# Attention in a hybrid layer: the products by the rows of reciprocal sums stand behind a visit's turned tiles and copies instead of behind its minima

## The chip, the core and the metric

The kernel runs on one core of a Trainium2 chip. The metric is the device time of one launch in microseconds. The core's engines run their own queues of instructions in order: TensorE (PE; its weight loads are shown as PEld), VectorE (DVE), ScalarE (ACT), GpSimd (POOL) and SyncE (SP). An instruction that waits for a semaphore holds all that is queued behind it on its engine. SP's queue issues most DMA transfers, POOL's and ACT's a few.

## The reference

One layer with two branches over the same 1024 tokens, all in float32, with 1024 channels: a projection of the normed input; branch A, a chunked state space scan (SSD); branch B, attention with a forget gate; two output projections, a merge by sigmoid gates, a last projection and a norm. What the change touches is branch B, 16 heads of 64:

```python
fcum = jnp.cumsum(log_f, axis=-1)
for blk in range(seqlen // ATT_BLOCK):
    q0, q1 = blk * ATT_BLOCK, (blk + 1) * ATT_BLOCK
    s = jnp.einsum('bhqd,bhkd->bhqk', q[:, :, q0:q1], k[:, :, :q1]) * scale
    s = s + fcum[:, :, q0:q1, None] - fcum[:, :, None, :q1]
    s = jnp.where(kpos[None, :] <= qpos[:, None], s, -jnp.inf)
    prob = jax.nn.softmax(s, axis=-1)
    outs.append(jnp.einsum('bhqk,bhkd->bhqd', prob, v[:, :, :q1]))
```

The output of each head is then multiplied by silu(z_att), the gate.

## The kernel before

**Stages.** After a prologue (norm and turned input, to about 100 us) a stream of matrix products runs to the end. Its products are made of seven products of combined blocks instead of eight (x0h to x6h in the rows; `raw` is a loaded weight block, `sum` a sum of two, `wop` its high and low parts). Into this stream the two branches are woven: the SSD groups to about 655 us, then the attention from 667 to 1143 us, then the output projections, the merge and the norm alone.

**Visits.** The attention handles its 16 heads as 8 pairs, hp 0 to 7 (both heads e of a pair lie on one tile's two halves of the partitions). A pair takes 6 visits g = 0 to 5, and visit m is 6 hp + g. A visit takes two blocks of 128 queries against one half h of 512 keys: (7, 6) half 1, (7, 6) half 0, (5, 4) half 1, (5, 4) half 0, (3, 2) and (1, 0) half 0. A set n of query blocks ends at an odd g: n = 0 at g = 1, n = 1 at g = 3 and n = 2 (the lower four blocks) at g = 5. `end(m)` gives the set that ends in visit m, if one does.

**One visit** m issues, in this order:

1. `scores`: for each of the four (block, head), PE makes s, DVE takes the row's minimum (L1526, a custom instruction and a read of its accumulator, into nm), ACT the exponential with its sum sm (L1530).
2. `out` of the set that ended two visits ago. For n = 0 and 1 it is DVE's product o*rb (L1491) and the sum of the two halves into zr (L1492); for n = 2 one product into zr (L1485). Behind n = 1 and n = 2, `outputs` stores zr to ya_dram by POOL (L1581) and makes differences for the output projections' blocks, on POOL for all pairs but the last (L1587, L1593, L1594, L1607), which are stored later as the stream's chores.
3. `weighted`: PE multiplies the previous visit's p by v into av.
4. For the set that ended one visit ago: `free`, DVE's o = av * gate (L1479), and `send`: PE turns ns (tp), ACT copies it (st, L1452), POOL stores it to st_dram (L1454).
5. For the set that ends here: `settle`, DVE's L1425 and two L1427 (the difference of the halves' minima, dd), and ACT's exponential of dd (L1428).
6. `fill(m, 0)`: a share of the stream's half steps (12 PE products each, with their weight splits on ACT L354 and DVE L356, sums L363, L379, evictions L410, L422 and the like).
7. For the set that ends here: `scale` (DVE L1439, L1440, the reciprocal L1441, ns at L1444; L1435 and L1436 for n = 2) and `load_gates` (SP loads zr from za_dram, L1466; there are two zr tiles).
8. `loads` of later tiles (v at L1399, q, k, and others), then `turned`: PE turns the exponentials (pt, L133), and the copies p leave PSUM by DVE (L1548, one block in four) or ACT (L1550).
9. For the set that ended one visit ago: `take`, SP's two loads of rb from st_dram, each row of reciprocal sums spread over 64 partitions (L1460).
10. `fill(m, 1)`: a second share of the stream.

The PSUM tiles s, pt and tp share four banks, so a visit's scores wait for the copies p of the visit before. `tc.high_priority()` and `pin` steer a list scheduler that sets each engine's order when the program is built; it goes by the order of issue and its own estimates of time. rb lies in a ring of four tiles that the stream's th tiles use too. Where a set ends in visit m, its tp is turned in m + 1, its rb asked for in m + 1, and its product made in m + 2. So the products stand in odd visits from m = 3 on.

Of the kernel before, what the change touches and what calls it, by code (L numbers as in the profile page):

```python
# [86 lines left out]
def hybrid_layer(ctx: ExitStack, tc, a, out):  # L87
# [1105 lines left out]
    with tc.tile_pool(name="pro", bufs=1, reuse_waits="tile", side="right") as pro, tc.tile_pool(  # L1193
# [44 lines left out]
        def turned(tiles, k):  # L1238
            pt = prop.tile([P, HALF], F32, tag="pt", bufs=3, name="pt")
            for j in range(4):  # L1240
                turn(pt[:, j * P : (j + 1) * P], tiles[j][:, k * P : (k + 1) * P]) 
            return pt
# [112 lines left out]
    with tc.tile_pool(name="att", bufs=1, reuse_waits="tile", side="right") as ap, tc.tile_pool(  # L1355
# [142 lines left out]
        def scores(hp, g, u):  # L1498

            pair, h = GROUPS[g]  # L1500
            i = pair[u]
            w = min(HALF, (i + 1) * P - h * HALF)
            s = [pp.tile([P, HALF], F32, tag="s", bufs=4, name="s") for e in range(2)]
            t, keys = q[hp, pair], k[hp, h]
            isl = slice(i % 2 * P, i % 2 * P + P)
            ops = [(t[:, x, isl], keys[:, y, 0:w]) for x, y in ((0, 0), (0, 1), (1, 0))]
            diagonal = h == i // 4
            for m, (x, y) in enumerate(ops):
                for e in range(2):
                    mm(  # L1510
                        s[e][:, 0:w], x[rows[e]], y[rows[e]], start=(m == 0), stop=(m == 2 and not diagonal),
                        skip_group_check=True,
                    )
            if diagonal:
                for n, (x, y) in enumerate(corner):
                    for e in range(2):
                        mm(
                            s[e][:, w - P : w], x[rows[e]], y[rows[e]], start=False, stop=(n == 1),
                            skip_group_check=True,
                        )  # L1520
            hd = heads[hp]
            for e in range(2):
                o = ex[:, e, u, 0:w]
                nm = hd.at(hd.nm, i, h, e)
                pin(
                    nc.vector.tensor_tensor_reduce(  # L1526
                        o, s[e][:, 0:w], fb[hp, h][:, e, 0:w], 1.0, 3.0e38, ALU.add, ALU.min, nm
                    )
                )
                pin(nc.scalar.activation(o, o, AF.Exp, scale=-1.0, bias=nm, accum_out=hd.at(hd.sm, i, h, e)))  # L1530
# [23 lines left out]
        def weighted(hp, g, b, first, p, start, stop):  # L1554
            pair, h = GROUPS[g]
            n = (7 - pair[0]) // 2 if pair[0] > 3 else 2
            hd = heads[hp]
            if n not in hd.av:
                hd.av[n] = pp.tile([P, HALF], F32, tag="av", bufs=1, name="av")
            c0 = 256 * h if n < 2 else pair[1] * P  # L1560
            for e in range(2):
                mm(
                    hd.av[n][rows[e], c0 + first * P : c0 + 256], v[hp, h][:, b % 4, rows[e]], p[:, e, first:, :],
                    start=start, stop=stop, skip_group_check=True,
                )
# [44 lines left out]
        def loads(m):  # L1610

            hp, g = divmod(m, 6)
            more = hp + 1 < NK
            if g == 0:
                if hp:
                    load_v(hp, 0)
                if hp < KH:
                    stream.chores += [None] + list(ops_s.differences(hp, difference_tile, small))
            if g == 1:
                load_q(hp, (3, 2))  # L1620
            if g == 2 and more:
                load_k(hp + 1, 1)
            if g == 3:
                load_q(hp, (1, 0))
                if more:
                    load_v(hp + 1, 1)
                if hp >= KH:
                    state["t"] = difference_tile()
                    nc.sync.dma_start(state["t"], ops_a.block("t1", hp - KH))
            if g == 4:  # L1630
                if more:
                    load_q(hp + 1, (7, 6))
                if hp >= KH:
                    state["y"] = fetched("b11", hp - KH)
            if g == 5 and more:
                load_k(hp + 1, 0)
                load_q(hp + 1, (5, 4))

        def end(m):

            hp, g = divmod(m, 6)
            if 0 <= hp < NK and g % 2:
                yield heads[hp], g // 2
# [15 lines left out]
        def fill(m, part):  # L1659
            share = weights[min(m // 6, NK - 1)] * rooms[m % 6][part]  # L1660
            to = stream.steps.index((ends[4], 6))
            stream.halves(round((2 * (to - stream.at) - (stream.run is not None)) * share / left[0]))
            left[0] -= share

        made = []
        for m in range(6 * NK + 1):

            stream.visit = m + 1
            hp, g = divmod(m, 6)
            if not g and hp < NK:  # L1670
                heads[hp] = Heads(hp)
            if m < 6 * NK:
                for u in range(2):
                    scores(hp, g, u)
            for hd, which in end(m - 2):
                hd.out(which)
            for one in made:
                weighted(*one)
            for hd, which in end(m - 1):
                hd.free(which)  # L1680
                if m < 6 * NK:
                    hd.send(which)
            stream.release()
            if m == 6 * NK:
                heads[NK - 1].out(2)
                stream.visit = 0
                break
            for hd, which in end(m):
                hd.settle(which)
            fill(m, 0)  # L1690

            for hd, which in end(m):
                hd.scale(which)
                hd.load_gates(which)
            loads(m)
            made = turned(hp, g)
            for hd, which in end(m - 1):
                hd.take(which)
            if m == 6 * NK - 1:
                heads[hp].send(2)  # L1700
            stream.hold()
            fill(m, 1)
            if m == 6 * NK - 1:
                heads[hp].take(2)
# [59 lines left out]
```

## Time and profile before

| | us |
|---|---|
| median of 3 runs | 1293.77 |
| the three runs | 1293.59, 1293.77, 1294.79 |
| the profiled execution, its own time | 1294.79 |
| its span | 1293.1 |
| granted TensorE clock, mean share of full | 0.997 |

The profiled execution is the slowest of the three. A row of the timeline reads: start, length, engine, line, operation, tiles (out<-in), shape, count, and in brackets the idle time of the engine ahead of it with what ended it. Idle time of an engine costs time only where the engine that sets the end waits in its turn. Other groups of instructions in the page's list, by busy time:

```profile
L356 DVE TENSOR_TENSOR wop<-sum,wop 128x512 fp32r<-128x512 f32 x174 | 140.5, 808 | 53.4 <-ACT wop L354 52.7
L1530 ACT ACTIVATE ex<-ex,nm 128x512 f32<-128x512 f32 (+1 forms) x192 | 116.1, 606 | 76.9 <-DVE nm L1526 75.7
L1526 DVE CUSTOM_DVE_ANT_0 ex<-s,fb 128x512 f32<-128x512 f32 (+1 forms) x192 | 96.8, 553 | 24.4 <-PE s L130 24.3
L130 PE MATMUL s<-k,q 64*128 64x512 f32 (+3 forms) x576 | 75.7, 373 | 6.2 <-DVE p L1548 4.4
```

Behind the first bar stand the busy time in us and the mean ns of one, behind the second the idle time of the engine ahead of the group, and what ended most of it.

### The profile page before, as it was taken

What the parts mean: (1) busy time and instruction counts of PE and PEld (TensorE: products, weight loads), DVE (VectorE), ACT (ScalarE), POOL (GpSimd) and SP (SyncE); (2) the same over time, 40 slices, a digit from 0 to 9 for tenths busy, and PEclk for the clock granted to TensorE, in tenths of its full rate; (3) what the DMA queues carried; (4) which work ended last, traced back from release to release, by engine and by line L of the source; (5) the groups of instructions that cost most, each with busy time, mean ns of one, the idle gap of its engine ahead of it and who ended that gap; (6) DMA issues with size and microseconds to landing.
All of it is one profiled execution on the core that took longest, in us unless ns stands there. A gap on an engine that the chain in (4) does not pass through costs nothing. (4 is left out here: it accounts for less than half of the span.)

```text
span 1293.1 us, 21078 instructions
## 1 busy us (share of the span) xinstructions
PE 1253.8 (97%) x7066; PEld 986.1 (76%) x7066; DVE 1014.7 (78%) x1979; ACT 794.3 (61%) x1728; POOL 284.6 (22%) x307
## 2 busy tenths in 40 slices
PE   6999999999999999899999999999999999999998
PEld 4787888788888888688776777777767777678786
DVE  6998888888789878788676766676789767876875
ACT  8755666466556756566555666566677556743654
POOL 0000330024102320143001222222121313256052
PEclk9999999999999999999999999999999999999999
DMA  7332543644363545445564657666677657665932
GB/s 281 104 106 71 154 148 121 199 140 146 127 210 116 153 153 164 122 154 154 168 237 153 221 175 224 193 208 196 228 282 250 219 178 253 230 219 189 364 112 102
DMA packets 154669, 233.60 MB, mean 181 GB/s; under 512 B 17216, under 2 KB 62656, under 8 KB 154560
## 3 DMA queue, kind: packets, MB, share of 16 engines
q1 hardware_dynamic: 142016, 205.53, 49.8%
q0 software_dynamic: 6400, 16.10, 3.3%
q10 hardware_dynamic: 6144, 10.62, 2.2%
q8 instruction: 56, 0.92, 0.3%
q14 instruction: 53, 0.43, 0.1%
HBM read 162.99 MB, written 72.34 MB: 182 GB/s over the span
## 5 line engine op out<-in xcount | busy, mean ns | idle before, releaser
L356 DVE TENSOR_TENSOR wop<-sum,wop 128x512 fp32r<-128x512 f32 x174 | 140.5, 808 | 53.4 <-ACT wop L354 52.7
L354 ACT ACTIVATE wop<-sum 128x512 fp32r<-128x512 f32 x174 | 108.8, 626 | 99.0 <-DVE sum L363 44.7
L1530 ACT ACTIVATE ex<-ex,nm 128x512 f32<-128x512 f32 (+1 forms) x192 | 116.1, 606 | 76.9 <-DVE nm L1526 75.7
L410 ACT ACTIVATE s<-pb 128x512 f32<-128x512 f32 x141 | 83.5, 592 | 97.3 <-PE pb L130 95.9
L130 PE MATMUL pc<-x3h,wop 128*128 128x512 f32 x384 | 131.6, 399 | 2.5 <-ACT wop L354 2.0
L130 PE MATMUL pb<-x0h,wop 128*128 128x512 f32 x384 | 132.2, 400 | 0.7 <-ACT x0h L1246 0.6
L130 PE MATMUL pc<-x2h,wop 128*128 128x512 f32 x384 | 131.4, 399 | 0.4 <-DVE u L422 0.4
L130 PE MATMUL pb<-x6h,wop 128*128 128x512 f32 x376 | 129.2, 399 | 1.6 <-ACT s L410 1.6
L130 PE MATMUL pb<-x5h,wop 128*128 128x512 f32 x376 | 128.3, 398 | 1.3 <-ACT s L410 1.3
L130 PE MATMUL pb<-x4h,wop 128*128 128x512 f32 x376 | 128.6, 398 | 0.2 <-DVE wop L356 0.2
L356 DVE TENSOR_TENSOR wop<-raw,wop 128x512 fp32r<-128x512 f32 x149 | 104.3, 702 | 29.8 <-ACT wop L354 29.5
L1526 DVE CUSTOM_DVE_ANT_0 ex<-s,fb 128x512 f32<-128x512 f32 (+1 forms) x192 | 96.8, 553 | 24.4 <-PE s L130 24.3
L354 ACT ACTIVATE wop<-raw 128x512 fp32r<-128x512 f32 x151 | 93.8, 623 | 15.8 <-PE pc L130 10.1
L130 PE MATMUL pd<-x1h,wop 128*128 128x512 f32 x264 | 89.1, 396 | 0.0
L130 PEld LDWEIGHTS pc<-x3h,wop 128*128 128x128 f32 x384 | 72.1, 188 | 20.2 <-issue 3.8
L130 PEld LDWEIGHTS pb<-x0h,wop 128*128 128x128 f32 x384 | 72.5, 189 | 17.2 <-ACT x0h L1246 1.3
L130 PEld LDWEIGHTS pc<-x2h,wop 128*128 128x128 f32 x384 | 72.1, 188 | 16.1 <-DVE u L422 0.8
L130 PEld LDWEIGHTS pb<-x6h,wop 128*128 128x128 f32 x376 | 70.6, 188 | 18.1 <-ACT s L410 2.7
L130 PEld LDWEIGHTS pb<-x5h,wop 128*128 128x128 f32 x376 | 70.6, 188 | 17.5 <-ACT s L410 2.2
L130 PEld LDWEIGHTS pb<-x4h,wop 128*128 128x128 f32 x376 | 70.5, 188 | 15.7 <-issue 0.7
L130 PE MATMUL s<-k,q 64*128 64x512 f32 (+3 forms) x576 | 75.7, 373 | 6.2 <-DVE p L1548 4.4
L214 POOL TENSOR_TENSOR wd<-wd 128x256 f32<-128x256 f32 x32 | 31.3, 978 | 228.3 <-DMA wd<-in_wo 125.7
(341 smaller groups left out, 3012.1 us busy)
## 6 DMA issues: line engine op xcount, KB each, us to landing
raw<-in_wu SPq DMA_DIRECT2D x128, 256.0 KB, 3.7
csb<-cs_dram SPq DMA_DIRECT2D x32, 256.0 KB, 5.5
fb<-f_dram SPq DMA_DIRECT2D x16, 512.0 KB, 6.5
rb<-st_dram SPq DMA_DIRECT2D x48, 128.0 KB, 3.2
wd<-in_wo SPq DMA_DIRECT2D x40, 128.0 KB, 3.1
xt<-in_x SPq DMA_DIRECT2D x8, 512.0 KB, 5.8
gs_dram<-th ACTq DMA_DIRECT2D x16, 256.0 KB, 3.4
qh_dram<-th SPq DMA_DIRECT2D x16, 256.0 KB, 5.2
```

The costliest lines, as they stand in the source:

```text
L130: return tc.keep_in_program_order(nc.tensor.matmul(*args, **kw))
L214: pin(nc.gpsimd.tensor_tensor(t[out_], t[a_], t[b_], ALU.subtract))
L354: nc.scalar.activation(op[:, 0], src, AF.Copy, scale=sign)
L356: nc.vector.tensor_tensor(op[:, 1], src, op[:, 0], ALU.subtract)
L410: nc.scalar.activation(s, ps, AF.Copy)
L1526: nc.vector.tensor_tensor_reduce(o, s[e][:, 0:w], fb[hp, h][:, e, 0:w], 1.0, 3.0e38, ALU.add, ALU.min, nm)
L1530: pin(nc.scalar.activation(o, o, AF.Exp, scale=-1.0, bias=nm, accum_out=hd.at(hd.sm, i, h, e)))
```

## The change

In a visit, `out` of the set that ended two visits ago is issued in step 2 only for the last head pair. For the others it is issued behind step 9, after the visit's turned tiles, their copies p and the loads of rb. Nothing else changes.

```diff
             for hd, which in end(m - 2):
-                hd.out(which)
+                if hd.last:
+                    hd.out(which)
...
             made = turned(hp, g)
             for hd, which in end(m - 1):
                 hd.take(which)
+            for hd, which in end(m - 2):
+                if not hd.last:
+                    hd.out(which)
             if m == 6 * NK - 1:
```

This concerns the 21 odd visits 3 to 43. PE's instructions keep their order. On DVE, in visit 3 (pair 0, the first visit with such a product), the queue behind the four minima was:

```order
L1491 TENSOR_TENSOR o<-o,rb 128x512
L1425 TENSOR_TENSOR nr<-nm 128x4
L1492 TENSOR_TENSOR zr<-o 128x256
L1427 TENSOR_TENSOR dd<-nr,nm 128x4 x2
L422 TENSOR_TENSOR th<-pc,s 128x512
L356 TENSOR_TENSOR wop<-sum,wop 128x512
L1439 TENSOR_TENSOR sm<-sm,dd 128x8
L379 TENSOR_TENSOR sum<-sum,raw 128x512
L669 SCALAR_TENSOR_TENSOR th<-th 128x512
L1440 TENSOR_TENSOR sm<-sm 128x4
L1441 RECIPROCAL sm<-sm 128x4
L1444 SCALAR_TENSOR_TENSOR ns<-dd,sm 128x8
```

Behind it came the copy p (L1548), a split (L356) and the next visit's minima. Now, behind the same four minima and then L1425 and L1427, it is:

```order
L422 TENSOR_TENSOR th<-pc,s 128x512
L1439 TENSOR_TENSOR sm<-sm,dd 128x8
L1440 TENSOR_TENSOR sm<-sm 128x4
L356 TENSOR_TENSOR wop<-sum,wop 128x512
L1441 RECIPROCAL sm<-sm 128x4
L669 SCALAR_TENSOR_TENSOR th<-th 128x512
L379 TENSOR_TENSOR sum<-sum,raw 128x512
L1444 SCALAR_TENSOR_TENSOR ns<-dd,sm 128x8
L1548 COPY p<-pt 128x512
L1491 TENSOR_TENSOR o<-o,rb 128x512
L356 TENSOR_TENSOR wop<-raw,wop 128x512
L1492 TENSOR_TENSOR zr<-o 128x256
```

The product and the sum have moved from the head of this piece to behind the copy p, and the next visit's minima follow them directly.

The scheduler also places other instructions anew. On DVE in visit 34 (pair 5, g = 4), where ns of the set that ended in visit 33 is made, the order from the visit's first minimum on was:

```order
L1526 ISA ex,nm<-s,fb 128x512
L1526 ISA nm 128x1
L1526 ISA ex,nm<-s,fb 128x512
L1526 ISA nm 128x1
L1444 SCALAR_TENSOR_TENSOR ns<-dd,sm 128x8
L1526 ISA ex,nm<-s,fb 128x384
L1526 ISA nm 128x1
L1526 ISA ex,nm<-s,fb 128x384
L1526 ISA nm 128x1
L379 TENSOR_TENSOR sum<-sum,raw 128x512
L1479 TENSOR_TENSOR o<-av,zr 128x512
```

and is now:

```order
L1526 ISA ex,nm<-s,fb 128x512
L1526 ISA nm 128x1
L1526 ISA ex,nm<-s,fb 128x512
L1526 ISA nm 128x1
L379 TENSOR_TENSOR sum<-sum,raw 128x512
L1441 RECIPROCAL sm<-sm 128x4
L1526 ISA ex,nm<-s,fb 128x384
L1526 ISA nm 128x1
L1526 ISA ex,nm<-s,fb 128x384
L1526 ISA nm 128x1
L1479 TENSOR_TENSOR o<-av,zr 128x512
L1444 SCALAR_TENSOR_TENSOR ns<-dd,sm 128x8
```

ns, which PE turns for `send`, has moved from behind the second minimum to behind the fourth, the sum and o<-av.

On ACT, in visit 33 (pair 5, g = 3), from the visit's first exponential on, it was:

```order
L1530 ACTIVATE ex,sm<-ex,nm 128x512 x4
L278 ACTIVATE x2h<-x2l 128x512 x2
L410 ACTIVATE s<-pb 128x512
L354 ACTIVATE wop<-sum 128x512
L1428 ACTIVATE dd<-dd 128x8
L1550 ACTIVATE p<-pt 128x512 x3
```

and is now:

```order
L1530 ACTIVATE ex,sm<-ex,nm 128x512 x3
L410 ACTIVATE s<-pb 128x512
L354 ACTIVATE wop<-sum 128x512
L1530 ACTIVATE ex,sm<-ex,nm 128x512
L278 ACTIVATE x2h<-x2l 128x512 x2
L1428 ACTIVATE dd<-dd 128x8
L1550 ACTIVATE p<-pt 128x512 x3
```

The fourth exponential has moved behind the eviction L410 and the split L354.

## The prediction

> **What bounds the kernel now.** I read the busy table of the page first, then the table of stretches, then what the TensorE (PE) and VectorE (DVE) waited for between 664 and 1150 us, and last the timeline at those waits. In the stretches the columns are start:end, length, busy time of PE, PEld, DVE, ACT and POOL, then the granted clock, the DMA share and GB/s.
>
> ```profile
> span 1293.1 us, 21078 instructions
> PE 1253.8 (97%) x7066; PEld 986.1 (76%) x7066; DVE 1014.7 (78%) x1979; ACT 794.3 (61%) x1728; POOL 284.6 (22%) x307
> 820.00:880.00 60.00, 59.94 (x408) 45.53 (x406) 40.54 (x103) 37.78 (x93) 13.95 (x18) 1.00 0.65 202
> 940.00:1000.00 60.00, 57.72 (x389) 43.05 (x387) 53.32 (x124) 46.38 (x114) 11.00 (x15) 1.00 0.80 277
> 704.00:710.00 6.00, 4.48 (x32) 2.94 (x34) 4.35 (x14) 3.45 (x9) 0.00 (x0) 0.72 0.17 60
> ```
>
> TensorE sets the end: it is busy for 97% of the span, and in 820 to 880 it lacks 0.06 us of 60. PE's own instructions and their order do not change, so the change can win or lose only idle time of PE and slow clock. Both sit in few places: 2.3 us are idle in 940 to 1000, where DVE is busy for 53.32 of 60 us, and the rest of the waits follow. What ended PE's idle time (engine, line, what it waited for: us in all, times, longest), and DVE's on the rows `rb`:
>
> ```profile
> PE s L130 <- DVE p L1548: 4.4, 4, 3.2
> PE s L130 <- ACT p L1550: 1.6, 5, 0.4
> PE tp L133 <- DVE nm L1526: 1.5, 2, 1.2
> PE tp L133 <- DVE ns L1444: 1.1, 1, 1.1
> DVE o L1491 <- DMA rb<-st_dram: 11.7, 8, 4.4
> ```
>
> Before the products of two heads DVE stands 11.7 us for rows that have not landed. PE loses far less by it; its longest wait, 3.2 us for a copy p, lies right behind the longest stand. Here it is, visit 3 (visit m is pair m // 6, part g = m % 6):
>
> ```profile
> 696.28 1.13 SPq L1460 DMA_DIRECT2D rb<-st_dram  x2
> 699.03 1.91 PE L133 MATMUL pt<-ident,ex 128*128 128x128 f32 x16
> 700.55 0.69 DVE L1491 TENSOR_TENSOR o<-o,rb 128x512 f32<-128x512 f32 x1 [4.37 <-DMA rb<-st_dram]
> 701.93 0.39 PE L130 MATMUL pb<-x6h,wop 128*128 128x512 f32 x1
> 704.07 1.56 ACT L1550 ACTIVATE p<-pt 128x512 f32<-128x512 f32 x3
> 704.78 0.68 DVE L1548 COPY p<-pt 128x512 f32<-128x512 f32 x1
> 705.52 1.65 PE L130 MATMUL s<-k,q 64*128 64x512 f32 x6 [3.21 <-DVE p L1548]
> ```
>
> The rows are asked for at 696.28 and used at 700.55; behind the product in DVE's queue stand the maxima's differences, a sum, two weight splits, the scale and the copy p at 704.78, which frees the PSUM bank that the next scores need. PE stops at 702.32 and starts at 705.52. Right behind it the clock row of 704 to 710 reads 0.72: it lacks 0.28 x 6 = 1.7 us of full clock, one half-clock period of about 3.4 us. From 820 to 880 it reads 1.00. So this one stand costs 3.2 + 1.7 = **4.9 us**.
>
> The Trainium skill, "TensorE: Matmul & The Clock Gate", section "Part 1: The HAM clock gate", has the clock halved after an idle window of about 3.4 us whose windows run free of the program. The gap of 3.21 us with one slow period behind it agrees, up to 0.2 us. The rule speaks against the change if a gap of that length opens elsewhere, by 1.7 us; R1 below prices such a gap from rows.
>
> **The change part by part.** Nothing is computed more or less. These products move, all but the last pair's:
>
> ```profile
> L1491 DVE TENSOR_TENSOR o<-o,rb x16: 685/691/694, 700.6 to 1128.5; 128x512 f32<-128x512 f32 x16
> L1492 DVE TENSOR_TENSOR zr<-o x16: 415/425/426, 701.3 to 1129.3; 128x256 f32<-128x256 f32 x16
> L1485 DVE TENSOR_TENSOR zr<-o,rb x8: 686/688/694, 740.0 to 1142.9; 128x512 f32<-128x512 f32 x8
> ```
>
> That is 14 pairs of 0.69 + 0.43 us and 7 single products of 0.69 us: 14 x 1.12 + 7 x 0.69 = 20.5 us of DVE time, the same before and after, in the 21 odd visits 3 to 43. They pass from behind the visit's minima to behind its copies p.
>
> *A, visit 3.* The minima end at 696.2, and the differences, the split and the scale now follow at once. I add their rows by hand: the scale ends at about 700.5, DVE's copy p at about 701.2, ACT's three by about 701.9 (1.56 us for three, behind PE's turns, which end at 700.94). PE finishes its last pb at 702.32, so the scores find free banks. The product, now behind p, finds rows that landed by 700.55. The gap goes and the half-clock period with it: **-4.9**. The least it can be is 0, if p gets a new cause (rival 2).
>
> *B, later stands.* Three more of PE's waits lie behind a product at the head of the queue: in visit 30 the turn tp of 958.86, in visit 21 one of the waits on ACT's copies (0.34 of the 1.6 above), in visit 43 the scores of 1096.48.
>
> ```profile
> 958.86 0.27 PE L133 MATMUL tp<-ident,ns 128*8 128x128 f32 x1 [1.24 <-DVE nm L1526]
> 1096.48 0.55 PE L130 MATMUL s<-k,q 64*128 64x128 f32 x6 [0.55 <-DVE p L1548]
> 964.71 1.29 DVE L282 TENSOR_TENSOR x5l<-x5l,x5h 128x512 fp32r<-128x512 f32 x2
> 972.76 2.57 DVE L282 TENSOR_TENSOR x5l<-x5l,x5h 128x512 fp32r<-128x512 f32 x2 [0.45 <-ACT x5h L281]
> 972.86 1.31 POOL L1607 TENSOR_TENSOR x<-x,zr 128x512 f32<-128x512 f32 x1
> ```
>
> 1.24 + 0.34 + 0.55 = **-2.1**, from 0 (the backlog stays) to -3.0 (with 0.9 of the 2.2 us that the rows on p and nm above have left). For visit 30 there is a second reason besides the stand. The last three rows show it: two subtractions take 1.29 us at 964.71, but 2.57 at 972.76, where POOL's difference L1607, which follows the product, begins a tenth of a us later. The minima read PSUM and do not stretch so. Behind the change POOL's followers start later and fall beside the next visit's minima. This loses 1.28 us each time it is met, and gains it where it is left.
>
> The Trainium skill, "SBUF — State Buffer", section "SBUF: two separate sides", calls that port pair an exclusive lock: of a GpSimd operation and a DVE operation with two SBUF inputs, the later one fully blocks. The trace agrees: 1.28 us more against POOL's 1.31. By the rule the moved o*rb products (two SBUF inputs themselves) could also block, which would cost up to 1.3 us each time a POOL operation runs behind p. With one such meeting the sum below would be 1.3 us smaller. In this kernel POOL's differences wait for just these products, so the sum stays.
>
> *C, visit 34, a loss.* In the new order ns of this visit stands behind all four large minima, the sum L379, a reciprocal and o<-av; before, it stood behind the second.
>
> ```profile
> 1002.14 0.16 DVE L1444 SCALAR_TENSOR_TENSOR ns<-dd,sm 128x8 f32<-128x8 f32 x1
> 1002.45 0.27 PE L133 MATMUL tp<-ident,ns 128*8 128x128 f32 x1 [1.09 <-DVE ns L1444]
> 1003.18 0.69 DVE L379 TENSOR_TENSOR sum<-sum,raw 128x512 f32<-128x512 f32 x1
> 1003.78 0.69 DVE L1479 TENSOR_TENSOR o<-av,zr 128x512 f32<-128x512 f32 x1
> ```
>
> PE already waits 1.09 us there for ns. Ahead of it now come what the rows show behind it there: two more minima up to 1003.18, L379 (0.69) and o<-av, which ends at 1003.78 + 0.69 = 1004.47, and a small reciprocal. ns would end at about 1004.75 instead of 1002.30 if DVE came as late as now: +2.45 us. DVE comes 0.5 to 1.5 us earlier, since it no longer stands for rows ahead of it nor stretches beside POOL. I take **+1.5**, from 0.3 to 2.45.
>
> *D, visit 33, a loss.* ACT's fourth exponential now stands behind L410 and L354, and the turns pt of that visit need it:
>
> ```profile
> 995.64 0.58 ACT L410 ACTIVATE s<-pb 128x512 f32<-128x512 f32 x1
> 996.12 0.62 ACT L354 ACTIVATE wop<-sum 128x512 fp32r<-128x512 f32 x1
> ```
>
> 0.58 + 0.62 = 1.20 us later at most; PE does not need all four exponentials at once, since it turns one block after the other, and the minima come earlier for the reason of C. I take **+0.4**, from 0 to 1.2.
>
> *E, the even visits that follow.* Product and sum (1.12 us) now stand ahead of the next visit's minima. Mostly DVE idles there for PE's scores; where it does not, the minima come later by at most 1.12 us, and the turn tp behind them, which waits in only three visits now (2 + 1 in the table), waits too. I count two visits, 36 and 42, where DVE has no idle time in front, and a few tenths in each: **+0.3**, from 0 to 1.0.
>
> *F, SP's queue.* The load of the next pair's gates into zr waits for the store of the old zr, which waits for the product. Where that load stands ahead of the load of v (into the pairs 1, 2, 3 and 7), v goes out later too. Here are SP's waits, the pairs 1, 2 and 3 in turn, and the landings of v (shortest, median, longest):
>
> ```profile
> SPq L1466 <- DMA ya_dram<-zr: 55.5, 12, 8.3
> 730.17 0.38 SPq L1399 DMA_DIRECT2D v<-v_dram  x1
> 737.15 1.73 PE L130 MATMUL av<-p,v 128*64 128x256 f32 x16
> 785.67 0.33 SPq L1466 DMA_DIRECT2D zr<-za_dram  x1
> 786.09 0.39 SPq L1399 DMA_DIRECT2D v<-v_dram  x1
> 794.42 1.73 PE L130 MATMUL av<-p,v 128*64 128x256 f32 x16
> 843.99 0.38 SPq L1399 DMA_DIRECT2D v<-v_dram  x1
> 852.45 1.73 PE L130 MATMUL av<-p,v 128*64 128x256 f32 x16
> DMA to landing us min/median/max: 3.4/4.0/5.9
> ```
>
> By the rows of p the product ends 3.2, 4.8 and 4.9 us later in these. If the store then takes as long as now, v goes out at 733.4, 790.9 and 848.9 and lands 4.0 later: 0.2 + 0.5 + 0.45 = 1.15 us behind the av that wants it. If the store lands sooner, there is no stall. I take half, **+0.6**, from 0 to 1.15; the longest landing is rival R3.
>
> Sum: -4.9 - 2.1 + 1.5 + 0.4 + 0.3 + 0.6 = **-4.2 us**. Against the profiled execution (1294.79 us, 1.7 over its span) that is 1290.6. The profiled execution is the slowest of the three shown, 1.0 over their median of 1293.77; on the median I get **1289.6 us**.
>
> **The rivals.** *R1, the gap moves to visit 34.* If C costs its full 2.45, the wait there is 1.09 + 2.45 = 3.5 us, as long as the gap of visit 3, and may bring a half-clock period of 1.7 us as that did: -4.9 - 2.1 + 2.45 + 1.7 + 0.4 + 0.3 + 0.6 = -1.55, or 1292.2. For it: ns really is moved behind all that. Against: DVE arrives earlier.
>
> *R2, the wait of visit 3 is only traded.* The scores there wait for four copies, and ACT's three end at 704.07 + 1.56 = 705.63, 0.2 us after DVE's. If ACT, which has its own splits and the exponential of the differences ahead of them, holds the banks as late as DVE did, A is 0: -2.1 + 1.5 + 0.4 + 0.3 + 0.6 = +0.7, 1294.5. Against it: ACT's exponential waits there for DVE's differences, so the stand of DVE is ACT's too.
>
> *R3, slower: v comes late.* If each v takes the longest landing of 5.9 in place of 4.0, the three stalls are 2.1 + 2.4 + 2.35 us, and pair 7 loses about 0.9: 7.75 in place of 0.6, so -4.2 + 7.15 = +3.0, 1296.8. It makes the kernel slower by over 0.2% once v is late by about (4.8 + 2.6) / 4 = 1.85 us a pair. For it: 55.5 us of zr's waits for stores, which all start later now, and PE's order is fixed, so a late v stops it. Against: it needs every landing near its longest.
>
> **How the numbers follow.** Forecast .62, R1 .17, R2 .11, R3 .10. A measurement here can tell about 0.2%, 2.6 us, from no change: faster is under 1291.2, slower over 1296.4. The forecast and a little of R1 (.02, with C between) give faster .64; the rest of R1 and R2 give same .26; R3 gives slower .10. The best by the bounds is -4.9 - 3.0 + 0.3 = -7.6, 1286.2, and I let 0.4 go below it for clock and spread: 1285.8. The worst of the forecast and R1 together is -7.0 + 2.45 + 1.7 + 1.2 + 1.0 + 1.15 = +0.5, 1294.3; R2 with F at its end is 1295.1. The range **1285.8 to 1295.1** holds all but R3 and some of the edges.
>
> **What the profile would show.** A: no bracket of 3 us on the scores of visit 3, the clock near 1.00 in the stretch 704 to 710, and no DVE wait for rb but in the last pair. B: no wait at the tp of visit 30. C: a wait of 1.5 to 3.5 us at the tp of visit 34, for ns; over 3.2 with a clock under 1.00 behind it is R1. D: a wait on exp at visit 33's pt. F: the first av of the pairs 1, 2 and 3 waits for v by some tenths; by 2 us it is R3. The prediction is wrong if PE's idle time in 664 to 1150 doesn't fall by about 2.5 us, or if PE waits there for a v in more than these places.

## The result and the profile after

The changed kernel is slower: 1298.99 us against 1294.05 (medians of 14 runs each), ratio 1.0039, 95% interval 1.0027 to 1.0051, so about 5 us. The profiled execution took 1296.91 us, the lowest of the 14 (they reach to 1303.22); its span is 2.1 us over that of the kernel before.

First the page's head, then what ended PE's idle time from 664 to 1160 us, and DVE's on `rb`:

```profile
span 1295.2 us, 21074 instructions
PE 1251.1 (97%) x7066; PEld 985.2 (76%) x7066; DVE 1013.6 (78%) x1979; ACT 794.0 (61%) x1728; POOL 286.6 (22%) x307
```

```profile
PE tp L133 <- DVE nm L1526: 6.8, 7, 1.5
PE pt L133 <- ACT ex L1530: 3.7, 6, 1.1
PE tp L133 <- DVE ns L1444: 3.0, 1, 3.0
PE s L130 <- ACT p L1550: 1.1, 2, 0.9
PE s L130 <- DVE p L1548: 1.1, 2, 0.9
```

```profile
DVE zr L1485 <- DMA rb<-st_dram: 1.4, 1, 1.4
```

DVE no longer stands for rows, but for one product of the last pair, and the wait of 3.2 us on the copy p is gone. In its place PE waits at the turns tp: 6.8 us in seven places for the minima, before 1.5 us in two, and 3.0 us for ns, before 1.1. The granted clock in the two stretches where it was or became low (columns as in the prediction; 0.91 over 20 us is, to the rounding, one half-clock period, which lacks 1.7 us):

```profile
700.00:720.00 20.00, 20.00 (x149) 15.45 (x148) 12.86 (x33) 12.41 (x33) 3.04 (x4) 1.00 0.56 182
1000.00:1020.00 20.00, 17.31 (x107) 13.48 (x109) 8.94 (x29) 9.56 (x26) 1.72 (x3) 0.91 0.55 172
```

A quick way to see where two kernels part is one instruction that both have in every part, here the turn tp of each set, and how much later it starts in the changed kernel:

| tp in visit | before, us | after, us | after minus before | PE's wait there, before and after |
|---|---|---|---|---|
| 2 | 687.38 | 687.84 | +0.46 | 0, 0 |
| 4 | 710.65 | 706.28 | -4.37 | 0, 0 |
| 6 | 728.30 | 725.23 | -3.07 | 0, 1.27 |
| 12 | 785.57 | 783.52 | -2.05 | 0, 1.01 |
| 18 | 843.60 | 841.67 | -1.93 | 0, 1.09 |
| 28 | 941.31 | 938.58 | -2.73 | 0, 0 |
| 30 | 958.86 | 956.35 | -2.51 | 1.24, 1.46 |
| 32 | 981.97 | 978.57 | -3.40 | 0, 0 |
| 34 | 1002.45 | 1002.69 | +0.24 | 1.09, 3.03 |
| 36 | 1020.09 | 1022.19 | +2.10 | 0, 0.44 |
| 46 | 1119.13 | 1121.35 | +2.22 | 0, 0 |

The changed kernel wins 4.8 us in visit 3, loses half of it again by visit 18, and more than all that was left between the visits 32 and 36.

What makes the waits of the visits 6, 12 and 18 stands in the timeline. Before, at visit 6:

```profile
725.23 1.29 POOL L214 TENSOR_TENSOR x<-x,th 128x512 f32<-128x512 f32 x1 [1.53 <-DMA th<-ys_dram]
726.54 0.69 DVE L356 TENSOR_TENSOR wop<-raw,wop 128x512 fp32r<-128x512 f32 x1
727.15 0.68 DVE L1526 CUSTOM_DVE_ANT_0 ex<-s,fb 128x512 f32<-128x512 f32 x1
728.30 0.27 PE L133 MATMUL tp<-ident,ns 128*8 128x128 f32 x1
```

and after:

```profile
722.12 0.58 POOL L1581 DMA_DIRECT2D ya_dram<-zr  x1 [11.06 <-DVE zr L1492]
722.34 2.23 DVE L356 TENSOR_TENSOR wop<-raw,wop 128x512 fp32r<-128x512 f32 x1
722.71 1.29 POOL L214 TENSOR_TENSOR x<-x,th 128x512 f32<-128x512 f32 x1
724.49 0.68 DVE L1526 CUSTOM_DVE_ANT_0 ex<-s,fb 128x512 f32<-128x512 f32 x1
725.23 0.27 PE L133 MATMUL tp<-ident,ns 128*8 128x128 f32 x1 [1.27 <-DVE nm L1526]
```

POOL's queue stands at the store of zr until the product is made (11.06 us), and its next operation L214, a difference of the other branch, starts 0.6 us behind the store. That is just when DVE makes its last split ahead of the minima. The split takes 2.23 us in place of 0.69, so the minima are late, and tp, which stands behind them, waits 1.27 us.

### The profile page after: what moved, and what is told of

The parts are those of the page before. It is cut to its first block, busy times and chain, and to the rows that moved or that the text cites. A ratio compares the mean times of both kernels' runs of the same rounds, so it can differ in the third digit from the quotient of the medians.

```text
span 1295.2 us, 21074 instructions
## 1 busy us (share of the span) xinstructions
PE 1251.1 (97%) x7066; PEld 985.2 (76%) x7066; DVE 1013.6 (78%) x1979; ACT 794.0 (61%) x1728; POOL 286.6 (22%) x307
## 5 line engine op out<-in xcount | busy, mean ns | idle before, releaser
L356 DVE TENSOR_TENSOR wop<-sum,wop 128x512 fp32r<-128x512 f32 x174 | 144.0, 828 | 54.7 <-ACT wop L354 54.2
L354 ACT ACTIVATE wop<-sum 128x512 fp32r<-128x512 f32 x174 | 108.7, 626 | 98.9 <-DVE sum L363 46.6
L410 ACT ACTIVATE s<-pb 128x512 f32<-128x512 f32 x141 | 83.5, 592 | 99.7 <-PE pb L130 98.5
L356 DVE TENSOR_TENSOR wop<-raw,wop 128x512 fp32r<-128x512 f32 x149 | 107.5, 723 | 33.3 <-ACT wop L354 32.8
L354 ACT ACTIVATE wop<-raw 128x512 fp32r<-128x512 f32 x151 | 93.8, 623 | 15.7 <-PE pc L130 10.0
L130 PEld LDWEIGHTS pb<-x0h,wop 128*128 128x128 f32 x384 | 72.9, 190 | 17.4 <-ACT x0h L1246 1.5
L214 POOL TENSOR_TENSOR wd<-wd 128x256 f32<-128x256 f32 x32 | 31.6, 989 | 226.9 <-DMA wd<-in_wo 120.9
L130 PE MATMUL pb<-x0l,wop 128*128 128x512 f32 x192 | 75.7, 394 | 0.7 <-DVE x0l L1248 0.7
```

Of the source, the lines that this page charges most:

```text
L130: return tc.keep_in_program_order(nc.tensor.matmul(*args, **kw))
L214: pin(nc.gpsimd.tensor_tensor(t[out_], t[a_], t[b_], ALU.subtract))
L354: nc.scalar.activation(op[:, 0], src, AF.Copy, scale=sign)
L356: nc.vector.tensor_tensor(op[:, 1], src, op[:, 0], ALU.subtract)
L410: nc.scalar.activation(s, ps, AF.Copy)
```

## The experiments

Theory P: POOL's operations, let go by the moved product, block DVE's last operation ahead of the next minima; and ns of visit 34 is late, with a half-clock period behind it. Each ratio is against the kernel before in the same session, with its 95% interval.

**1. The changed kernel again**, with no edit.

> The changed kernel once more, unaltered, for a second profile and for times beside the others on one chip. Theory P (POOL's operations, let go by the moved product, block DVE's last split ahead of the next minima; and ns of visit 34 late with a half-clock period behind it): 1299, 5 us over the kernel before, with waits of 1.0 to 1.5 us at tp of the visits 6, 12, 18, 30 and 44 and of about 3 us at visit 34. Theory Q (the excess is made elsewhere, by DMA in the stages outside the attention): the waits vary between the profiles and do not add up.

1298.57 us, ratio 1.0038 (1.0019 to 1.0056). The waits come back in the same places, to 0.5 us each (tp for minima 6.5 us in seven places, for ns 3.0). Q falls. Its profile also has a half-clock period that the other one lacks (see the end).

**2. The products of n = 1 back.**

```diff
-                if hd.last:
+                if not (not hd.last and which != 1):
                     hd.out(which)
...
-                if not hd.last:
+                if not hd.last and which != 1:
                     hd.out(which)
```

> Only the products of n = 1 (in the visits with g = 5, the ones whose store and differences POOL takes up) go back behind the minima; n = 0 and n = 2 stay moved. Theory P: the tp waits of the visits 6, 12, 18 and 30 go (together 4.9 us of waits, some 2 to 3 us net), that of visit 34 stays: 1296 to 1297. If the product's 1.1 us on DVE is what delays the minima, and not POOL: the same here, so this run bounds the share of n = 1 alone. If neither: no difference from the changed kernel, 1299.

1296.83 us, ratio 1.0027 (1.0014 to 1.0039): 1.7 us better than run 1, but the two intervals overlap, so the times alone do not tell the two apart. The tp waits of the visits 6, 12 and 18 are gone (0, 0 and 0.01 us). That of visit 20 stays, 0.41 us: its product has n = 2, which is still moved and has POOL's work behind it too. That of visit 30 stays, 1.7 us, a miss. With the product back in its old place POOL's L1593 falls on other operations of DVE: two subtractions L279 ahead of the minima take 2.53 us, where run 3, with POOL's work later, has 1.29. Visit 34 waits 4.0 us for ns, and four half-clock periods are in this profile, so that the time comes out as expected is in part luck.

**3. POOL's work later.** `out` no longer calls `outputs`; a method `post` does, one visit later for all pairs but the last.

```diff
                 if m < 6 * NK:
                     hd.send(which)
+            for hd, which in end(m - 3):
+                if which and not hd.last:
+                    hd.post(which)
```

> All products stay where the change puts them; only what POOL does behind them (the store of zr and the differences) is issued one visit later, behind the send of the next set, for all pairs but the last. Theory P: DVE's split ahead of the minima of the visits 6, 12, 18 and 30 takes 0.7 us again in place of 1.7 to 2.2, and the tp waits there fall to 0.3 or less: 1296. The rival, that the product and its sum themselves (1.1 us) delay the minima: the waits stay at 1.0 us or more: 1299.

1296.76 us, ratio 1.0026 (1.0010 to 1.0041). This run tells the block from the product's own time, by its trace. Ahead of visit 12's minima DVE does the same instructions in the changed kernel:

```profile
778.97 0.68 DVE L1491 TENSOR_TENSOR o<-o,rb 128x512 f32<-128x512 f32 x1
779.68 0.42 DVE L1492 TENSOR_TENSOR zr<-o 128x256 f32<-128x256 f32 x1
781.00 1.30 POOL L214 TENSOR_TENSOR x<-x,th 128x512 f32<-128x512 f32 x1
781.17 1.69 DVE L356 TENSOR_TENSOR wop<-raw,wop 128x512 fp32r<-128x512 f32 x1 [1.06 <-ACT wop L354]
783.52 0.27 PE L133 MATMUL tp<-ident,ns 128*8 128x128 f32 x1 [1.01 <-DVE nm L1526]
```

and in this one, where POOL has done L214 by 775.3:

```profile
778.17 0.68 DVE L1491 TENSOR_TENSOR o<-o,rb 128x512 f32<-128x512 f32 x1
778.89 0.42 DVE L1492 TENSOR_TENSOR zr<-o 128x256 f32<-128x256 f32 x1
780.37 0.69 DVE L356 TENSOR_TENSOR wop<-raw,wop 128x512 fp32r<-128x512 f32 x1 [1.06 <-ACT wop L354]
781.73 0.27 PE L133 MATMUL tp<-ident,ns 128*8 128x128 f32 x1
```

The product stands where the change put it, the split waits the same 1.06 us for ACT, and it takes 0.69 us again: tp does not wait. For the visits 6, 12, 18 and 20 the rival falls. The one wait of tp on minima that is left is that of visit 36, 0.3 us (all of them were 6.5 in run 1); there the product and its sum stand ahead of the minima and nothing is stretched, so it is the product's own time. PE's waits in this kernel, whose line numbers are 4 higher:

```profile
PE pt L133 <- ACT ex L1534: 5.3, 10, 1.4
PE s L130 <- DVE p L1552: 2.6, 5, 1.8
PE tp L133 <- DVE ns L1444: 2.1, 1, 2.1
```

From the first tp to the last PE idles 9.9 us, in run 1 14.1. The time fell by only 1.8 us, again within the overlap of the intervals. Two things stand against the gain. New waits came up in the visits 31 to 34, the largest of them by the same block at a new place:

```profile
954.30 2.92 DVE L282 TENSOR_TENSOR x1l<-x1l,x1h 128x512 fp32r<-128x512 f32 x2
955.35 1.31 POOL L1597 TENSOR_TENSOR x<-zr,x 128x512 f32<-128x512 f32 x1
961.50 1.03 PE L130 MATMUL s<-k,q 64*128 64x512 f32 x4 [1.76 <-DVE p L1552]
```

Two such subtractions take 1.28 us at 959.56; the copy p that the scores wait for stands behind them in DVE's queue. And the profile has four half-clock periods, where run 1's has two; the mean granted clock of the 12 runs is 0.9953, of the 8 of run 1 0.9961, of the kernel before 0.9970.

**4. ns of visit 34 early.** `made` is the instruction at L1444.

```diff
-                for u in range(2):
-                    scores(hp, g, u)
+                with tc.issue_after(heads[hp].made.ins) if m == 34 else nullcontext():
+                    for u in range(2):
+                        scores(hp, g, u)
```

> The changed kernel with one edge of order more: in visit 34 the minima are issued behind ns. Nothing else moves but the sum and the reciprocal with it. Theory P with R1: the 3.0 us wait at tp and the half-clock period behind it (1.7 us) go, 3 to 4.7 us: 1294.3 to 1296. If PE then waits for something else there (the minima are 0.35 us later): less than 1.5 us gained, over 1297.5.

1295.23 us, ratio 1.0014 (1.0002 to 1.0025): 3.3 us better than run 1, by one edge of order, and clear of the interval of the changed kernel's 14 runs (1.0027 to 1.0051). The wait at tp falls from 3.0 to 0.9 us, now for the minima, and the clock reads 1.00 there (0.91 in the changed kernel):

```profile
1000.50 0.17 DVE L1444 SCALAR_TENSOR_TENSOR ns<-dd,sm 128x8 f32<-128x8 f32 x1
1001.33 0.27 PE L133 MATMUL tp<-ident,ns 128*8 128x128 f32 x1 [0.92 <-DVE nm L1526]
```

```profile
1000.00:1020.00 20.00, 18.13 (x132) 13.55 (x129) 12.00 (x36) 9.68 (x26) 3.79 (x7) 1.00 0.57 193
```

**5. Only visit 3's product moves.**

```diff
-                if hd.last:
+                if not (hd.hp == 0 and which == 0):
                     hd.out(which)
...
-                if not hd.last:
+                if hd.hp == 0 and which == 0:
                     hd.out(which)
```

> Only the one product of visit 3 moves; the other 20 stay behind the minima. What the prediction put under A, alone: the 3.2 us wait of the scores at 705 goes and the 1.7 us of half clock behind it, and nothing else changes: 1289 to 1290.6 against 1293.8. If the half-clock period only falls on another place in most runs: 1290.6. If the gap is only traded for another wait: 1293.8.

1290.24 us, ratio 0.9975 (0.9959 to 0.9991): faster than before, by 3.5 us. The wait of 3.2 us is gone from PE's list, where the rest stands much as before; the half-clock period of this profile lies at 955 instead.

```profile
PE s L130 <- DVE p L1548: 1.2, 3, 0.7
PE tp L133 <- DVE nm L1526: 1.2, 2, 0.9
PE tp L133 <- DVE ns L1444: 1.1, 1, 1.1
```

**6. Run 5 with ns of visit 34 early**, the edits of 4 and 5 together.

> As e5, and visit 34's minima are issued behind ns. The wait of 1.1 us at the tp of visit 34, which the kernel before has too, should go or fall under 0.3: 1288 to 1289.5. If DVE's minima, 0.3 us later, make PE wait at the turns instead: as e5.

1291.12 us, ratio 0.9976 (0.9963 to 0.9989), as run 5. The tp of visit 34 waits 0.7 us for the minima in place of 1.1 for ns, and nothing is won that these runs can tell: the second expectation.

**7. Runs 3 and 4 together.**

> e3 and e4 together: POOL's store and differences a visit later, and ns of visit 34 early. If the two losses are separate, they add up: tp waits under 0.4 us everywhere, 1293 to 1295, near the kernel before. If the visits 29 to 34 are bound by DVE and ACT whatever the order, the time only moves to pt and s there: 1295 to 1296.5.

1295.28 us, ratio 1.0017 (1.0006 to 1.0029), the last of the expectations. The tp waits are 2.8 us again in four places, pt waits 5.1 us for ACT and s 2.6 us for DVE. The two losses do not add up. In the visits 29 to 34 a delay taken away at one place comes up at the next: L282 takes 2.92 us beside POOL's L1597 here too, and the scores behind it wait 1.8 us at 963.

**8. Only n = 0 moves**, in all pairs but the last (the condition is `not hd.last and which == 0`).

> Only the products of n = 0 move (in the visits with g = 3); POOL does nothing behind these. Theory P: they cost nothing in the pairs 1 to 4, since no operation of POOL follows them, the gain of visit 3 stays; visit 34's ns is behind all minima here too and may cost 1 to 2.5 us: 1290 to 1293. The rival, that a product in front of the next minima costs its own 1.1 us whatever POOL does: tp waits in the visits 10, 16, 22 and 28, and 1294 or more.

1293.40 us, ratio 0.9996 (0.9986 to 1.0006). No tp waits in the visits 10, 16, 22 and 28: moved products without POOL's work behind them cost nothing there, though they stand ahead of the next minima. Visit 34 waits 2.9 us and has a half-clock period (999.5 to 1003), which uses up the gain of visit 3. Against the changed kernel (1.0039, 1.0027 to 1.0051) the ratio is 0.43% lower, some 5.5 us, and the intervals are apart: so much did it cost to move the products of n = 1 and 2 as well, those with POOL's work behind them.

```profile
PE tp L133 <- DVE ns L1444: 2.9, 1, 2.9
PE pt L133 <- ACT ex L1530: 2.6, 6, 1.1
PE tp L133 <- DVE nm L1526: 1.2, 2, 1.0
```

**9. n = 0 moves in the pairs 0 to 4 only** (`hd.hp < 5 and which == 0`).

> The products of n = 0 move in the pairs 0 to 4 only; in the pairs 5 to 7 and for n = 1 and 2 everything stays as in the kernel before. Visit 34 keeps ns behind its second minimum, with its wait of 1.1 us. Theory P: the gain of e5 and none of the losses, 1289 to 1290.5. If n = 0's products cost something in the pairs 1 to 4 after all: over 1291.

1290.30 us against 1295.13 in that session, ratio 0.9962 (0.9947 to 0.9978), the lowest of all, though its interval does not set it apart from the runs 5, 6 and 10. No wait is left in the visits 2 to 28 that is over 0.3 us, and this profile has no half-clock period before the last matmuls.

```profile
span 1285.4 us, 21084 instructions
PE tp L133 <- DVE ns L1444: 1.1, 1, 1.1
```

**10. Run 8 with ns of visit 34 early.**

> As e8 (n = 0 moves in all pairs but the last), with ns of visit 34 ahead of that visit's minima. If the 2.9 us wait and the half-clock period behind it are what e8 lost against e5: 1289 to 1290.5. If the other waits of the visits 29 to 34 grow in its place: 1291.5 to 1293.4.

1290.32 us, ratio 0.9970 (0.9956 to 0.9984). The wait for ns is gone (1.3 us for minima is left), and with it what run 8 lost against run 5. So the late ns of visit 34 turned the moved n = 0 from a gain into nothing; the intervals of the runs 8 and 10 are apart.

## Why the prediction was wrong

The prediction's own sign of being wrong came: PE's idle time in 664 to 1150 did not fall by 2.5 us but rose by 4.6, from 12.7 to 17.4.

**A was right in its mechanism.** From visit 2 to visit 4 the shift of tp in the table changes by 4.83 us, against 4.9; the gap and its half-clock period are gone, and no wait took their place, so R2 did not come. The rows added by hand came out too: the scale ends at 700.53 (700.5), DVE's copy p at 701.23 (701.2), ACT's three at 702.25 (701.9). (One reading was off: ahead of that copy one weight split stands behind the product, not two.) Alone A is worth 3.5 us (run 5), the gap without the half-clock period: the mean granted clock is 0.9974 in the 9 runs of run 5 and 0.9971 in the 32 before, which is 0.4 us, not 1.7. The 1.7 had been read from one profile, and in other runs the period falls elsewhere.

**E was the step that failed, and with it the sentence on the lock.** It gave +0.3 us with 1.0 as its end. In the profile tp waits 1.27 + 1.01 + 1.09 + 0.40 us in the visits 6, 12, 18 and 20, 0.44 in 36 and 1.16 in 44: 5.4 us. Of these only visit 36 is what E counted, the product's own time ahead of the minima. In the others DVE is blocked beside POOL; in visit 44 it is ns, just ahead of the minima, that takes 1.60 us in place of 0.15 beside L1607, which follows the moved product. The prediction had the lock and its price (1.28 us each time), and it dismissed it: "POOL's differences wait for just these products, so the sum stays". That they wait for them is what fixes where they fall: behind the store, 0.6 us after it, on DVE's next operation, and that one now stands right ahead of the minima. POOL's L214, which needs nothing of the product, was held in the queue behind the store and fell there too. Run 3 shows it for the visits 6 to 20, and run 8 gives the price of all the moves with POOL behind them. The claim in B that POOL's followers would "fall beside the next visit's minima" was wrong by that one microsecond, but for visit 36.

The Trainium skill, "SBUF — State Buffer", section "SBUF: two separate sides", has whichever of the two operations starts first hold the ports, and the other blocked fully. The trace agrees in size: 2.23 and 1.69 us in place of 0.69 beside POOL operations of 1.29 and 1.30. Which of the two was first cannot be read from the rows: at visit 6 DVE's split starts 0.37 us ahead of L214 and is still the one that is late, and the two rows that the prediction took as agreeing (972.76 and 972.86) have DVE first as well. The ends are plainer: in the visits 6, 12, 18, 20 and 30 DVE's operation ends 0.56 or 0.57 us after POOL's, wherever it starts. The prediction weighed the rule with one such meeting; the profile has six that PE waits behind (visits 6, 12, 18, 20, 30 and 44).

**C was forecast in the middle of its bounds, and the trace came nearer the upper end.** +1.94 us of wait (3.03 in place of 1.09) against +1.5, and the half-clock period of R1, +1.7, which had .17. DVE did come earlier, as argued, by 2.0 us at the first minimum of visit 34 (998.95 in place of 1000.92), but so did PE, whose av ends 1.7 us earlier. Run 4 gives 3.3 us for both together.

**D**: pt of visit 33 waits 0.94 us in place of 0.13, +0.81 against +0.4, inside its bounds. Not forecast at all: the scores of visit 33 wait 0.89 us for ACT's copies p of visit 32, and its cause stays open.

**B**: of -2.1 only 0.9 came, and visit 44 took that back. The waits behind the copies of visit 21 (0.34) and 43 (0.55) went, but visit 30 waits 1.46 us in place of 1.24. B put that wait down to the stand for rows in the visit before, which is only 0.31 us long, and showed for its second reason rows at 964.71 and 972.76, which lie behind the wait at 958.86. The meetings with POOL that lie ahead of it begin with this one, before:

```profile
952.53 2.52 DVE L279 SCALAR_TENSOR_TENSOR x4l<-x4l,x4h 128x512 fp32r<-128x512 f32 x2
953.19 1.30 POOL L1593 TENSOR_TENSOR x<-zr,x 128x512 f32<-128x512 f32 x1
```

and after, on another operation of DVE (2.09 us in place of 0.69):

```profile
953.59 2.09 DVE L387 TENSOR_TENSOR raw<-raw 128x512 f32<-128x512 f32 x1
953.84 1.28 POOL L1593 TENSOR_TENSOR x<-zr,x 128x512 f32<-128x512 f32 x1
```

In run 3, with POOL's work later, tp of visit 30 waits 0.06 us.

**F and R3 did not come.** In no place does PE wait for v; zr's load waits 30.6 us for stores in place of 55.5, and v's longest landing is 5.0 us in place of 5.9:

```profile
SPq L1466 <- DMA ya_dram<-zr: 30.6, 9, 6.2
DMA to landing us min/median/max: 3.0/4.6/5.0
```

**The sum.** Without A's gap of 3.2 us, PE's waits of 0.15 us and more between the first tp and the last grew from 6.9 to 14.2 us: visits 6 to 20 3.8 us, 30 0.2, 33 1.7, 34 1.9, 36 0.4, and 44 0.6 (its 1.16 less the 0.55 that its scores waited before), less some 1.3 us of small waits that went. With the half-clock period of visit 34, 1.7 us, that is 9.0 us. By the medians it is 4.9 + 3.5 (what run 5 wins) = 8.4. The two spans give less, 2.1 + 4.5 = 6.6: in the profile after, PE's busy time is 2.7 us shorter than before (1251.1 and 1253.8 us) for the same 7066 products. Why was not settled.

## What to carry to other kernels

Before an instruction is moved on one engine, follow what it lets go on the others, the whole queue behind the one that waits and not only the ones that use its result, and look at which DVE operation will then run beside POOL. A stall of DVE is worth only what PE loses behind it: of 11.7 us of standing for rows 3.2 reached PE in one place, and little elsewhere; moving one or five of the 21 products won 3.5 to 5 us, where all 21 lost 5. Where a scheduler places the rest, compare the order around the tightest visits: one small instruction (ns, 0.16 us) behind two more minima made some 3 us.

## What the runs showed of the hardware

The half-clock periods do not need a long gap. Each is about 3.4 us long and lacks 1.71 us. Those of the runs stand behind PE gaps of 3.21 us (visit 3 before), 3.03 and 2.94, but also of 1.77 (run 7, at 963), 1.70 (run 4, at 1117) and 1.68 (run 2, at 1117), and in run 5 behind two of 0.69 and 0.94 us at 952 and 955. And the length of a gap does not decide: at 534 one of 1.94 us in run 3 brought a period, and one of 1.99 at 535 in the kernel before did not. Here are the same stretches of the changed kernel, first of its first profile, then of run 1's, which is the same program:

```profile
542.00:546.00 4.00, 2.67 (x14) 2.31 (x15) 4.00 (x8) 2.27 (x4) 0.12 (x1) 1.00 0.66 129
1002.00:1006.00 4.00, 3.31 (x10) 2.69 (x11) 0.54 (x2) 1.06 (x5) 1.14 (x2) 0.57 0.22 85
```

```profile
542.00:546.00 4.00, 3.19 (x10) 2.74 (x11) 4.00 (x8) 2.14 (x6) 0.63 (x2) 0.57 0.60 117
1002.00:1006.00 4.00, 3.69 (x11) 2.98 (x12) 0.16 (x2) 0.68 (x3) 1.14 (x2) 0.64 0.12 45
```

At 543 PE waits 2.6 us in the one and 2.8 in the other; only the second has the clock at 0.57 behind it. The profiles held none to four such periods. So a wait of 1.7 us, or two shorter ones close together, can cost its own length and, in some runs, 1.7 us besides, and the times of one program scatter by a few us. It can blur a comparison too: the mean granted clock is 0.9970 in the 31 runs of the kernel before that stand beside the runs 1 to 4, but 0.9945 in the 11 of run 2 and 0.9953 in the 12 of run 3, which is 3.2 and 2.2 us of slow clock more. Why these two kernels meet more such periods stays open.

The Trainium skill, "TensorE: Matmul & The Clock Gate", section "Part 1: The HAM clock gate", has windows that run free of the program, which fits the difference between the two profiles of one program. It puts the halving behind an idle window of about 3.4 us; here gaps of half that length had it, and the measurement decides.
